# SiLU and GELU as single ScalarE functions in a hybrid decoder layer, with the stores of ScalarE's last results on ScalarE's queue

## The chip, the cores and the metric

The kernel runs on 1 core of one Trainium2 chip. The metric is device time in microseconds of one execution. The engines are named as in the profile: PE is TensorE's matmul stream and PEld its weight loads, DVE is VectorE, ACT is ScalarE, POOL is GpSimd, SP is SyncE, which here only issues DMAs. SPq and ACTq are the instruction streams of SP and ACT where they issue DMAs or wait. Each engine works through its own stream in program order.

## The reference

One layer on a sequence of 2048 tokens with 1024 channels, all in float32:

```python
h = rmsnorm(x, norm_w[i])
proj = h @ w_in[i]
u, z_s, q, k, v, z_a = jnp.split(proj, splits, axis=-1)      # 512 columns each
# s5_branch(u): state-space layer, 32 groups of 16 channels, 64 complex states each
y = y.reshape(bsz, s_len, SSM_WIDTH) + d_skip * uf
y = jax.nn.gelu(y)                                            # tanh form
y = y * jax.nn.sigmoid(y @ glu_w + glu_b)
y_s = y_s * jax.nn.silu(z_s)
# diff_attention(q, k, v): 4 heads, two 64-dim maps each, QK-norm, rotary, sub-norm
y_a = y_a * jax.nn.silu(z_a)
x = x + jnp.concatenate([y_s, y_a], axis=-1) @ w_out[i]
x = x + jax.nn.sigmoid(x @ ple_w_gate[i]) * (p[i] @ ple_w_proj[i])
```

silu(z) is z * sigmoid(z), which equals 0.5 * z * (1 + tanh(z/2)). gelu here is 0.5 * y * (1 + tanh(sqrt(2/pi) * (y + 0.044715 y^3))).

## The kernel before

Products in full precision are made from three passes: each operand is split into a rounded high part and the rest (names ending in h and l), and high x high, high x low and low x high are summed in PSUM. ACT makes the high part with a copy, DVE or POOL the low part with a subtraction.

There are three phases. **Phase 1**, up to about 722 us, makes the input projection and the whole state-space branch. **Phase 2**, up to about 1157 us, is attention, head by head, with the first half of the output projection as filler. **Phase 3** is the second half of the output projection, the gate and the residual.

In phase 1 the foreground loop goes over twelve blocks of 512 weight columns: u for both halves of the sequence, then for the first half k, zs, v, q, za, and for the second half zs, k, v, q, za. Each block goes over four tiles `t` of 256 tokens. Eight weight chunks of a block come in as `wraw` by a DMA that ACT's queue issues (L279), ACT scales and rounds them to `wh` (L282), DVE makes `wl` (L283). Blocks zs and u put channels on partitions (matmuls at L781, 256 columns), the others tokens (L827, 512 columns). The foreground then makes

- zs: DVE scales PSUM by the norm (L797, L806), ACT takes tanh (L799, L809), DVE finishes SiLU (L800, L810), SP stores to `zs_scr` (L801, L811). Tiles t 0 and 3 are stored one channel block at a time (128x256), tiles 1 and 2 two at a time (128x512).
- v: ACT scales, SP stores to `v_scr` (L834, L835).
- za: ACT scales (L838) and takes tanh (L840), DVE finishes (L841), ACT's queue stores to `za_scr` (L842).
- q, k: QK-norm and rotary on DVE and POOL, ACT and DVE make high and low parts into `stg` (L870, L871), SP stores both (L874, L875).

Between the tiles a generator, `ssm`, is advanced by a number of steps per tile that a list, `BGP`, gives; this is the background. Its second part goes over 32 state-space groups: `U` is loaded (L598), scaled on POOL (L599) and split; PE multiplies it (L530 into `pss`); DVE rotates, scans and rotates back with tables `tab` (L636 to L647) with copies on ACT between (L637, L638); ACT and DVE split the states into `xah`, `xal`; PE multiplies again; ACT copies the result to the one buffer `ysb` (L655) and SP stores it to `yg_scr` (L656). After each eighth group SP issues eight rearranging DRAM to DRAM copies `y_scr<-yg_scr` (L659), which need these stores. Every four groups DVE also makes the next parameters and tables (`tx`, one buffer, stored to `tab_scr` at L563; `rs`, stored to `r_scr` and read back as `M`, L578 and L582).

The third part of `ssm`, called the GLU here, goes over eight pieces of 256 tokens: `y` is loaded into a tile named `gg` (L693); ACT squares it (L696), DVE makes the cubic argument (L697), ACT takes tanh (L698), DVE finishes GELU (L699), ACT and DVE or POOL split it (L700, L701); PE multiplies by `gwh` and `gwl` (L710); ACT takes the tanh of the gate (L717), DVE multiplies (L718) and then multiplies by the SiLU gate, loaded back from `zs_scr` into `gz` (two buffers, L715, L721); SP stores to `yt_scr` (L722).

The tile framework's scheduler puts the instructions of all engines in order at build time by a timing model of its own, with the background at lower priority; the waits that tiles and DRAM tensors need are added to that order. So an edit in one place can move instructions elsewhere.

Of the kernel before, what the change touches and what calls it, by code (L numbers as in the profile page):

```python
# [24 lines left out]
L = 8  # L25
# [9 lines left out]
GK = math.sqrt(2.0 / math.pi)  # L35
GS = math.sqrt(0.044715)
ONE_MINUS = 0.8
# [18 lines left out]
GTB = 5  # L56
# [62 lines left out]
def hymba_kernel(ctx, tc, x_t, p_t, positions, norm_w, w_in, lam_re, lam_im, log_dt, b_re, b_im,  # L119
                 c_re, c_im, ssm_d, glu_w, glu_b, q_norm_w, k_norm_w, lq1, lk1, lq2, lk2,  # L120
                 subln_w, w_out, w_proj, w_gate, out):
    nc = tc.nc
    V, A, G, T = nc.vector, nc.scalar, nc.gpsimd, nc.tensor
# [74 lines left out]
    with ExitStack() as p1:  # L198
# [114 lines left out]
        def ssm():  # L313

            with tc.tile_pool(name="p1s", bufs=1) as sp:
# [50 lines left out]

                V.tensor_scalar(subw, subw, float(np.float32(ONE_MINUS)) * 0.5, None, op0=ALU.mult)
# [144 lines left out]
            with tc.tile_pool(name="ssB", bufs=2) as sp:  # L512
# [102 lines left out]
                for g in range(NG):  # L615
# [35 lines left out]
                    def behind(g=g, py=py, w=[w_[:, gs] for w_ in wc4], xa=xa):  # L651
# [4 lines left out]
                        nc.sync.dma_start(yg_scr[g].rearrange("l p c -> (l p) c"), ysb)  # L656
# [12 lines left out]
            with tc.tile_pool(name="ssC", bufs=1) as pg:  # L669
# [13 lines left out]
                for cq in range(8):  # L683
# [7 lines left out]
                    for k in range(4):  # L691
                        y = g2[k]
                        nc.sync.dma_start(y.rearrange("q (l c) -> q l c", l=L), y_scr[k * 128:k * 128 + 128, :, c0:c0 + 32])  # L693
                        t = pg.tile([128, 256], F32, name="gt", bufs=GTB)

                        A.activation(t, y, AF.Square, scale=GS)  # L696
                        V.scalar_tensor_tensor(t, t, 1.0, y, op0=ALU.add, op1=ALU.mult)  # L697
                        A.activation(t, t, AF.Tanh, scale=GK)  # L698
                        V.scalar_tensor_tensor(g2[k], t, 1.0, y, op0=ALU.add, op1=ALU.mult)  # L699
# [4 lines left out]
                    for mp in range(2):  # L704
# [7 lines left out]
                        for e in range(2):  # L712
# [4 lines left out]
                            A.activation(th, pm[:, e, :], AF.Tanh, bias=gb[:, m:m + 1], scale=0.25)  # L717
# [3 lines left out]
                            V.scalar_tensor_tensor(zv, th.rearrange("q (l c) -> q l c", l=L), 0.125, zv, op0=ALU.mult, op1=ALU.mult)  # L721
# [17 lines left out]
        for bi, (hf, kind, c0) in enumerate(blocks):  # L739
            leaving = bi == len(blocks) - 1 or blocks[bi + 1][0] != hf  # L740
            for t in range(4):
# [5 lines left out]
                if kind in ("u", "zs"):  # L747
# [25 lines left out]
                    for cb, k in order:  # L773
# [20 lines left out]
                        elif t in KOUT:  # L794

                            zz = pt.tile([128, 512], F32, name="t2")[:, :256]
                            V.tensor_tensor(zz, pm, rbc[hf][:, t * 256:t * 256 + 256], op=ALU.mult)  # L797
                            zo = pt.tile([128, 512], F32, name="t2")[:, :256]
                            A.activation(zo, zz, AF.Tanh, scale=0.5)  # L799
                            V.scalar_tensor_tensor(zo, zo, 1.0, zz, op0=ALU.add, op1=ALU.mult)  # L800
                            nc.sync.dma_start(zs_scr[cb * 128:(cb + 1) * 128, tok:tok + 256], zo)  # L801
                        elif cb % 2 == 1:

# [4 lines left out]
                            zo = pt.tile([128, 512], F32, name="t2")  # L808
                            A.activation(zo, zz, AF.Tanh, scale=0.5)  # L809
                            V.scalar_tensor_tensor(zo, zo, 1.0, zz, op0=ALU.add, op1=ALU.mult)  # L810
                            nc.sync.dma_start(  # L811
                                zs_scr[(cb - 1) * 128:(cb + 1) * 128, tok:tok + 256].rearrange("(b q) t -> q b t", q=128),
                                zo.rearrange("q (b t) -> q b t", b=2))
# [3 lines left out]
                else:  # L817
# [3 lines left out]
                    for j in range(2):  # L821
# [577 lines left out]
```

## Time and profile before

| what | value |
|---|---|
| median of 3 runs | 1454.8 us (1452.43 to 1457.49) |
| profiled execution, its own time | 1451.3 us |
| its span | 1449.6 us |
| mean granted TensorE clock | 0.992 of full speed |

The span goes from the first to the last instruction of the profiled execution; its own time is 1.7 us above it. Of phases 1 to 3, only phase 1 holds the lines that are changed, and the largest stretch of it is the 32 groups (about 190 to 505 us) and the GLU (about 505 to 665 us).

### The profile page before, as it was taken

Reading aid. Unit: us, or ns where it says so; the run is one execution under the profiler, and the core shown is the slowest. Engines: PE = TensorE matmul, PEld = TensorE weight load, DVE = VectorE, ACT = ScalarE, POOL = GpSimd, SP = SyncE. Lnnn points to the kernel's source line nnn. Section 1 sums busy time; section 2 is a strip of 40 time slices with the busy share of each in tenths; the row PEclk is TensorE's granted clock in tenths of the full one; section 3 lists DMA queues with packets and bytes.
Section 4 is the critical chain, followed back from the end, with each engine's and each line's share of the span. In section 5 each row is a group of like instructions: output and inputs, shape, how many; then the busy total and the mean of one; then the engine's idle time right before and its main releaser. Section 6 shows DMA issues by size and latency. Waiting matters only on the chain.

```text
span 1449.6 us, 27391 instructions
## 1 busy us (share of the span) xinstructions
PE 1383.4 (95%) x9602; PEld 1270.7 (88%) x9602; DVE 1066.3 (74%) x2527; ACT 767.9 (53%) x1689; POOL 521.3 (36%) x670
## 2 busy tenths in 40 slices
PE   7899899899999999999899999999998999999998
PEld 7898798778798888887699899989898999999998
DVE  8588898799798866675577867777877448666754
ACT  8443345456554555453586777767787523322231
POOL 6632500144000421331144454454434335543440
PEclk9999999999999999999999999999999999999999
DMA  7549756546765386556864653655434365132221
GB/s 248 152 109 293 209 178 191 166 145 191 245 192 165 107 240 186 138 150 203 240 176 121 164 143 117 162 149 142 127 88 161 138 231 227 59 117 81 73 74 59
DMA packets 219410, 230.34 MB, mean 159 GB/s; under 512 B 62712, under 2 KB 168328, under 8 KB 216712
## 3 DMA queue, kind: packets, MB, share of 16 engines
q1 hardware_dynamic: 203144, 199.22, 45.8%
q10 hardware_dynamic: 16128, 29.37, 6.6%
q8 instruction: 75, 1.23, 0.4%
q14 instruction: 63, 0.52, 0.1%
HBM read 152.19 MB, written 84.72 MB: 163 GB/s over the span
## 4 chain that ended last, share of the span: by engine, by line
PE 37%; DVE 5%; ACT 3%; issue 2%; DMA 2%; POOL 1%; SPq 0%; DVEq 0%; ACTq 0%; POOLq 0%
PE pg L1265 11%; PE po L1102 7%; PE pmf L931 6%; PE pss L1066 6%; PE pl L1281 3%; PE ptw L1098 3%; ACT s L1077 2%; DVE wgt L1157 1%; DVE s L1068 1%; PE pm L931 1%; DVE s L1090 1%; DMA wgr<-in_ple_w_gate_dram 1%; DVE wg L1153 0%; DMA yt_scr<-yo 0%; DMA yin<-yt_scr 0%
## 5 line engine op out<-in xcount | busy, mean ns | idle before, releaser
L827 PE MATMUL pmm<-wh,xh 128*128 128x512 f32 x512 | 198.3, 396 | 3.9 <-ACT wh L282 2.8
L827 PE MATMUL pmm<-wl,xh 128*128 128x512 f32 x512 | 200.4, 395 | 0.0
L827 PE MATMUL pmm<-wh,xl 128*128 128x512 f32 x512 | 200.0, 393 | 0.0
L1066 PE MATMUL pss<-ks,qd 128*128 128x512 f32 (+3 forms) x640 | 185.8, 388 | 10.3 <-DVE st L1068 6.3
L1077 ACT ACTIVATE s<-s,st 128x1024 f32<-128x1024 f32 (+4 forms) x192 | 171.7, 899 | 37.9 <-DVE st L1068 33.1
L1265 PE MATMUL pg<-oph,wg 128*128 128x256 f32 x896 | 164.4, 286 | 3.0 <-ACT oph L1238 2.9
L1102 PE MATMUL po<-vt,wt 128*128 128x128 f32 x1088 | 152.7, 276 | 0.8 <-ACT yo L1114 0.7
L1102 PEld LDWEIGHTS po<-vt,wt 128*128 128x128 f32 x1088 | 142.2, 192 | 7.2 <-ACT yo L1114 0.9
L1265 PEld LDWEIGHTS pg<-oph,wg 128*128 128x128 f32 x896 | 141.5, 195 | 3.4 <-ACT oph L1238 3.4
L1068 DVE CUSTOM_DVE_ANT_0 s<-pss,mk,st 128x512 f32<-128x512 f32 (+2 forms) x192 | 121.7, 652 | 24.3 <-PE pss L1066 22.9
L781 PE MATMUL pmm<-xh,wl 128*128 128x256 f32 x448 | 127.2, 287 | 2.7 <-DVE wl L283 2.6
L1265 PE MATMUL pg<-opl,wg 128*128 128x256 f32 x448 | 127.2, 285 | 1.2 <-POOL opl L1239 1.2
L781 PE MATMUL pmm<-xh,wh 128*128 128x256 f32 x448 | 123.0, 288 | 5.3 <-DVE stg L791 1.5
L781 PE MATMUL pmm<-xl,wh 128*128 128x256 f32 x448 | 125.8, 284 | 0.0
L1066 PEld LDWEIGHTS pss<-ks,qd 128*128 128x128 f32 x640 | 100.4, 192 | 22.8 <-DVE st L1068 11.6
L827 PEld LDWEIGHTS pmm<-wh,xh 128*128 128x128 f32 x512 | 96.1, 188 | 25.3 <-ACT wh L282 5.7
L827 PEld LDWEIGHTS pmm<-wl,xh 128*128 128x128 f32 x512 | 96.5, 188 | 19.2 <-DVE wl L283 1.5
L827 PEld LDWEIGHTS pmm<-wh,xl 128*128 128x128 f32 x512 | 96.5, 189 | 18.6
L931 PE MATMUL pmf<-yh,woh 128*128 128x256 f32 x352 | 104.8, 298 | 4.7 <-DVE x L1188 3.8
L1068 DVE CUSTOM_DVE_ANT_0 s<-pss,mk 128x512 f32<-128x512 f32 (+3 forms) x128 | 78.6, 630 | 34.3 <-PE pss L1066 28.6
L931 PE MATMUL pmf<-yh,wol 128*128 128x256 f32 x352 | 99.8, 284 | 0.0
L931 PE MATMUL pmf<-yl,woh 128*128 128x256 f32 x352 | 99.6, 283 | 0.0
(385 smaller groups left out, 3822.6 us busy)
## 6 DMA issues: line engine op xcount, KB each, us to landing
wraw<-in_w_in_dram ACTq DMA_DIRECT2D x96, 256.0 KB
xraw<-in_x_t_dram SPq DMA_DIRECT2D x40, 256.0 KB
tab<-tab_scr SPq DMA_DIRECT2D x64, 136.0 KB
qd<-qh_scr SPq DMA_DIRECT2D x64, 128.0 KB
qd<-ql_scr SPq DMA_DIRECT2D x64, 128.0 KB
xr<-in_x_t_dram SPq DMA_DIRECT2D x32, 256.0 KB
yin<-yt_scr SPq DMA_DIRECT2D x16, 512.0 KB
xp_scr<-xp SPq DMA_DIRECT2D x32, 256.0 KB
```

Source lines behind the costliest of these rows:

```text
L781: T.matmul(pm, lhsT=w[b_][:, cb * 128:cb * 128 + 128], rhs=xt[a_][:, k, :], start=(k == 0 and n == 0), stop=(k == 7 and n == 2))
L827: T.matmul(pm, lhsT=xt[a_][:, k, j * 128:j * 128 + 128], rhs=w[b_], start=(k == 0 and n == 0), stop=(k == 7 and n == 2))
L931: T.matmul(pm[:, e, :], lhsT=w[k][b_][:, ms], rhs=y[a_][:, k, :], start=(k == 0 and n == 0), stop=(k == 3 and n == 2))
L1066: T.matmul(pss[:, :cl], lhsT=qd[:, e, m, tq], rhs=ks[m][:, c0:c0 + cl], start=e == 0, stop=e == 1)
L1068: V.tensor_tensor_reduce(sr[m][pi][:, o:o + cl], pss[:, :cl], mk[:, end - cl:end], scale=1.0, scalar=3.4e38 if ci == 0 else st[:, 2 * ci - ...
L1077: A.activation(sr[m][pi][:, :cl], sr[m][pi][:, :cl], AF.Exp, bias=st[:, ci + m:ci + m + 1], scale=-1.0, accum_out=st[:, 12 + 2 * pi + m:13 ...
L1090: V.scalar_tensor_tensor(s0, s1, st[:, 11:12], s0, op0=ALU.mult, op1=ALU.add)
L1098: T.transpose(ptw[:, k, :], blocks_[kg + k], ident)
L1102: T.matmul(po[:, 0:128], lhsT=wt[:, k, :], rhs=vt[:, kg + k, :], start=kg + k == 0, stop=kg + k == len(blocks_) - 1)
L1157: V.tensor_tensor(t_, a_, b_, op=ALU.subtract)
L1265: T.matmul(banks[mp][:, e], lhsT=wg[n][k][b_][:, m * 128:m * 128 + 128], rhs=x_[a_][:, k], start=k == 0 and q == 0, stop=k == 3 and q == 2)
L1281: T.matmul(banks[mp][:, e], lhsT=wp[k][b_][:, m * 128:m * 128 + 128], rhs=p_[a_][:, k], start=(k == 0 and q == 0), stop=(k == 1 and q == 2))
```

## The change

zs: the tanh and the DVE product become one ACT function, `Silu`, in place; the store goes to ACT's queue. The tile for the second result is gone. za of the first half: `Silu` straight from PSUM with the norm as its scale. za of the second half stays with tanh, with the scale halved by a small POOL operation. GELU: the square, the two DVE products and the tanh become one ACT function, `Gelu_apprx_tanh`, in place; the constants of the gate and the sub-norm are adapted, since zs and za are no longer twice SiLU. The stores of `yg_scr`, `zs_scr`, `v_scr` and of the high parts of q and k go from SP's queue to ACT's.

```diff
-                V.tensor_scalar(subw, subw, float(np.float32(ONE_MINUS)) * 0.5, None, op0=ALU.mult)
+                V.tensor_scalar(subw, subw, float(np.float32(ONE_MINUS)), None, op0=ALU.mult)
...
                         A.copy(ysb, py)
-                        nc.sync.dma_start(yg_scr[g].rearrange("l p c -> (l p) c"), ysb)
+                        nc.scalar.dma_start(yg_scr[g].rearrange("l p c -> (l p) c"), ysb)
...
-                        A.activation(t, y, AF.Square, scale=GS)
-                        V.scalar_tensor_tensor(t, t, 1.0, y, op0=ALU.add, op1=ALU.mult)
-                        A.activation(t, t, AF.Tanh, scale=GK)
-                        V.scalar_tensor_tensor(g2[k], t, 1.0, y, op0=ALU.add, op1=ALU.mult)
+                        A.activation(y, y, AF.Gelu_apprx_tanh)
                         A.copy(gh[k], g2[k])
...
-                            A.activation(th, pm[:, e, :], AF.Tanh, bias=gb[:, m:m + 1], scale=0.25)
+                            A.activation(th, pm[:, e, :], AF.Tanh, bias=gb[:, m:m + 1], scale=0.5)
...
                             V.tensor_tensor(zz, pm, rbc[hf][:, t * 256:t * 256 + 256], op=ALU.mult)
-                            zo = pt.tile([128, 512], F32, name="t2")[:, :256]
-                            A.activation(zo, zz, AF.Tanh, scale=0.5)
-                            V.scalar_tensor_tensor(zo, zo, 1.0, zz, op0=ALU.add, op1=ALU.mult)
-                            nc.sync.dma_start(zs_scr[cb * 128:(cb + 1) * 128, tok:tok + 256], zo)
+                            A.activation(zz, zz, AF.Silu)
+                            nc.scalar.dma_start(zs_scr[cb * 128:(cb + 1) * 128, tok:tok + 256], zz)
...
-                            nc.sync.dma_start(v_scr[rows, :], vo)
+                            nc.scalar.dma_start(v_scr[rows, :], vo)
                         elif kind == "za":
-                            zz = pt.tile([128, 512], F32, name="t2")
-                            A.activation(zz, pm, AF.Copy, scale=rstd[:, ti:ti + 1])
                             zo = pt.tile([128, 512], F32, name="t2")
-                            A.activation(zo, zz, AF.Tanh, scale=0.5)
-                            V.scalar_tensor_tensor(zo, zo, 1.0, zz, op0=ALU.add, op1=ALU.mult)
+                            if hf == 0:
+                                A.activation(zo, pm, AF.Silu, scale=rstd[:, ti:ti + 1])
+                            else:
+                                rsth = pt.tile([128, 16], F32, name="qst")
+                                G.tensor_scalar(rsth[:, j:j + 1], rstd[:, ti:ti + 1], 0.5, None, op0=ALU.mult)
+                                zz = pt.tile([128, 512], F32, name="t2")
+                                A.activation(zz, pm, AF.Copy, scale=rsth[:, j:j + 1])
+                                A.activation(zo, zz, AF.Tanh)
+                                V.scalar_tensor_tensor(zo, zo, 1.0, zz, op0=ALU.add, op1=ALU.mult)
                             nc.scalar.dma_start(za_scr[rows, :], zo)
...
-                        nc.sync.dma_start(hi_s[:, :, tok:tok + 256].rearrange("h q t -> q h t"), sh_.bitcast(F32))
+                        nc.scalar.dma_start(hi_s[:, :, tok:tok + 256].rearrange("h q t -> q h t"), sh_.bitcast(F32))
```

The 128x512 stores of zs are changed in the same way as the 128x256 ones.

The first place is ACT's stream where the GLU begins (row text: line, operation, out<-in, size of the output). Of before:

```order
L680 CAST gwh<-gg 128x256
L696 ACTIVATE gt<-gg 128x256
L279 DMA wraw<-in_w_in_dram 128x512
L696 ACTIVATE gt<-gg 128x256 x2
L279 DMA wraw<-in_w_in_dram 128x512
L696 ACTIVATE gt<-gg 128x256
L698 ACTIVATE gt<-gt 128x256 x4
L700 CAST gh<-gg 128x256 x4
```

and of the change, where lines are numbered anew (`gg<-gg` at L692 is the GELU, L693 the copy to the high part, L838 the square of the QK-norm):

```order
L677 CAST gwh<-gg 128x256
L692 ACT_TABLE_LOAD
L692 ACTIVATE gg<-gg 128x256
L693 CAST gh<-gg 128x256
L692 ACTIVATE gg<-gg 128x256
L693 CAST gh<-gg 128x256
L692 ACTIVATE gg<-gg 128x256
L838 ACTIVATE t_7009<-pmm,rstd 128x512
L693 CAST gh<-gg 128x256
```

One table load has come in ahead of the first GELU, and each GELU is followed by its copy, with no DVE result between them. In ACT's whole stream there are 7 table loads against 5: this one, and one ahead of the first exponential of phase 2.

The second place is SP's stream at the rearranging copies after the 24th group. Of before:

```order
L656 DMA yg_scr<-ysb 128x256
L602 DMA tab<-tab_scr_98 64x544
L659 DMA y_scr<-yg_scr 128x1x256 x8
L656 DMA yg_scr<-ysb 128x256
L563 DMA tab_scr_99<-tx 128x544
L578 DMA r_scr_68<-rs 128x64
L602 DMA tab<-tab_scr_98 64x544 x2
L582 DMA M<-r_scr_68 128x8x64
L811 DMA zs_scr<-t_6103 128x2x256
L811 DMA zs_scr<-t_6157 128x2x256
```

and of the change (L656 is now the copies, L575 and L579 the store and the load of `r_scr`):

```order
L599 DMA tab<-tab_scr_98 64x544 x2
L656 DMA y_scr<-yg_scr 128x1x256 x8
L575 DMA r_scr_68<-rs 128x64
L560 DMA tab_scr_99<-tx 128x544
L599 DMA tab<-tab_scr_98 64x544
L579 DMA M<-r_scr_68 128x8x64
L599 DMA tab<-tab_scr_98 64x544
L595 DMA U<-ug_scr 128x256
```

The stores of ACT's results are gone from SP; the copies, the store of `rs` and the load of `M` stay, and `r_scr` now follows the copies at once.

The third place is ACT's stream in the first zs block and the groups beside it, of the change (L790 and L797 are Silu, L791 and L798 its stores, L652 and L653 the copy to `ysb` and its store):

```order
L797 ACTIVATE t_3030<-t_3030 128x512
L634 COPY sw<-pss 64x256
L635 ACTIVATE sw<-pss 64x256
L521 CAST xah<-md 128x256
L798 DMA zs_scr<-t_3030 128x2x256
L521 CAST wah<-pss 128x512
L652 COPY ysb<-pss 128x256
L653 DMA yg_scr<-ysb 128x256
L797 ACTIVATE t_3082<-t_3082 128x512
```

Before, the same piece had no DMA in it. The stores stand up to three instructions behind the result that they store, among the copies of the rotation.

## Rows read from the trace of the kernel before

**Rows 1.** The page's first part: busy time, share of the span, instructions.
```profile
PE 1383.4 (95%) x9602; PEld 1270.7 (88%) x9602; DVE 1066.3 (74%) x2527; ACT 767.9 (53%) x1689; POOL 521.3 (36%) x670
```

**Rows 2.** Busy time by stretch: PE, PEld, DVE, ACT, POOL; clock, DMA share, GB/s.
```profile
150.00:505.00 355.00, 335.26 (x2008) 292.11 (x2007) 308.68 (x689) 184.83 (x391) 79.09 (x93) 1.00 0.59 179
505.00:665.00 160.00, 155.43 (x881) 133.90 (x880) 109.33 (x247) 81.05 (x188) 44.87 (x48) 1.00 0.65 180
```

**Rows 3.** Waits of PE from 150 to 505 us: total, times, longest.
```profile
PE pss L530 <- ACT ysb L655: 3.2, 3, 2.6
PE pss L530 <- DVE wal L525: 3.1, 1, 3.1
PE pss L530 <- DVE xal L525: 2.9, 6, 0.8
PE ptr L868 <- DVE stg L871: 2.0, 1, 2.0
...
PE pmm L781 <- DVE wl L283: 1.8, 2, 1.1
```

**Rows 4.** Waits of PE from 505 to 665 us: total, times, longest.
```profile
PE pss L710 <- ACT gh L700: 2.1, 2, 1.6
PE pss L710 <- POOL gl L701: 1.1, 1, 1.1
PE pmm L827 <- ACT wh L282: 1.1, 2, 0.7
```

**Rows 5.** Groups in phase 1: shapes, count, busy us, mean ns, idle before.
```profile
L699 DVE SCALAR_TENSOR_TENSOR gg<-gt,gg 128x256 f32<-128x256 f32 x32 | 13.2, 448 | 0.7 <-ACT gt L698 0.4
L697 DVE SCALAR_TENSOR_TENSOR gt<-gt,gg 128x256 f32<-128x256 f32 x32 | 13.0, 442 | 0.6 <-ACT gt L696 0.2
...
L841 DVE SCALAR_TENSOR_TENSOR t<-t,t 128x512 f32<-128x512 f32 x16 | 11.0, 688 | 8.4 <-ACT t L840 8.4
...
L800 DVE SCALAR_TENSOR_TENSOR t<-t,t 128x256 f32<-128x256 f32 x16 | 7.1, 446 | 0.0
...
L810 DVE SCALAR_TENSOR_TENSOR t<-t,t 128x512 f32<-128x512 f32 x8 | 5.5, 683 | 0.0
...
L696 ACT ACTIVATE gt<-gg 128x256 f32<-128x256 f32 x32 | 11.8, 415 | 9.3 <-DVE gz L721 7.5 <-DMA gg<-y_scr 1.0 <-DVE gg L699 0.7
...
L840 ACT ACTIVATE t<-t 128x512 f32<-128x512 f32 x16 | 10.1, 630 | 2.3 <-DMA tab<-tab_scr 2.1
```

**Rows 6.** Timeline at the second GLU piece, DVE and PE: start, duration, idle before.
```profile
543.63 0.62 DVE L721 SCALAR_TENSOR_TENSOR gz<-gt,gz 128x256 f32<-128x256 f32 x1 [5.63 <-DMA gz<-zs_scr]
544.16 0.76 DVE L699 SCALAR_TENSOR_TENSOR gg<-gt,gg 128x256 f32<-128x256 f32 x2
...
545.07 0.50 PE L710 MATMUL pss<-gh,gwh 128*128 128x256 f32 x2 [1.65 <-ACT gh L700]
```

**Rows 7.** Timeline of SP after the 8th group, and of DVE and PE behind it.
```profile
269.73 2.65 SPq L659 DMA_DIRECT2D y_scr<-yg_scr  x4
272.48 0.40 SPq L656 DMA_DIRECT2D yg_scr<-ysb  x1
272.98 0.37 SPq L563 DMA_DIRECT2D tab_scr<-tx  x1
...
278.66 0.72 DVE L558 TENSOR_TENSOR tx<-pt 128x544 f32<-128x544 f32 x1 [7.29 <-DMA tab_scr<-tx]
...
280.74 0.36 PE L530 MATMUL pss<-Uh,wah 128*128 128x256 f32 x1 [3.06 <-DVE wal L525]
```

**Rows 8.** Timeline of SP and PE after the 24th group.
```profile
439.66 5.45 SPq L659 DMA_DIRECT2D y_scr<-yg_scr  x8
445.21 0.40 SPq L656 DMA_DIRECT2D yg_scr<-ysb  x1
445.71 0.37 SPq L563 DMA_DIRECT2D tab_scr<-tx  x1
446.18 0.41 SPq L578 DMA_DIRECT2D r_scr<-rs  x1
...
455.33 0.39 PE L530 MATMUL pss<-Uh,wah 128*128 128x256 f32 x1 [2.60 <-ACT ysb L655]
```

**Rows 9.** The stores that ACT issues already: duration ns min/median/max.
```profile
L842 ACTq DMA_DIRECT2D za_scr<-t x16: 326/326/352, 364.4 to 714.0; - x16
```

**Rows 10.** Timeline of ACT at a table load, and at the first exponential of phase 2.
```profile
184.66 0.38 ACT L638 ACTIVATE sw<-pss 64x256 f32<-64x256 f32 x1
185.05 1.28 ACT L799 ACT_TABLE_LOAD   x1
186.35 0.42 ACT L799 ACTIVATE t<-t 128x256 f32<-128x256 f32 x1
...
684.69 0.40 ACT L1077 ACTIVATE s<-s,st 128x128 f32<-128x128 f32 x1 [4.23 <-DVE st L1068]
```

**Rows 11.** Waits of ACT from 150 to 665 us, the longest.
```profile
ACT wh L282 <- DMA wraw<-in_w_in_dram: 39.8, 23, 5.8
```

More of the change, by code (lines that the diff above doesn't have):

```diff
@@ L34 @@
 TWO_PI = 2.0 * math.pi
-GK = math.sqrt(2.0 / math.pi)
-GS = math.sqrt(0.044715)
 ONE_MINUS = 0.8
@@ L693, in ssm @@
                         nc.sync.dma_start(y.rearrange("q (l c) -> q l c", l=L), y_scr[k * 128:k * 128 + 128, :, c0:c0 + 32])
-                        t = pg.tile([128, 256], F32, name="gt", bufs=GTB)
-                        A.activation(t, y, AF.Square, scale=GS)
-                        V.scalar_tensor_tensor(t, t, 1.0, y, op0=ALU.add, op1=ALU.mult)
-                        A.activation(t, t, AF.Tanh, scale=GK)
-                        V.scalar_tensor_tensor(g2[k], t, 1.0, y, op0=ALU.add, op1=ALU.mult)
+                        A.activation(y, y, AF.Gelu_apprx_tanh)
                         A.copy(gh[k], g2[k])
@@ L716, in ssm @@
                             th = pg.tile([128, 256], F32, name="gt", bufs=GTB)
-                            A.activation(th, pm[:, e, :], AF.Tanh, bias=gb[:, m:m + 1], scale=0.25)
+                            A.activation(th, pm[:, e, :], AF.Tanh, bias=gb[:, m:m + 1], scale=0.5)
                             V.scalar_tensor_tensor(th, th, 1.0, g2[m], op0=ALU.add, op1=ALU.mult)
                             zv = zs.rearrange("q (c l) -> q l c", l=L)
-                            V.scalar_tensor_tensor(zv, th.rearrange("q (l c) -> q l c", l=L), 0.125, zv, op0=ALU.mult, op1=ALU.mult)
+                            V.scalar_tensor_tensor(zv, th.rearrange("q (l c) -> q l c", l=L), 0.5, zv, op0=ALU.mult, op1=ALU.mult)
                             nc.sync.dma_start(yt_scr[cq][m * 128:m * 128 + 128, :], zs)
@@ L807, in hymba_kernel @@
                                             rbc[hf][:, t * 256:t * 256 + 256].unsqueeze(1).to_broadcast([128, 2, 256]), op=ALU.mult)
-                            zo = pt.tile([128, 512], F32, name="t2")
-                            A.activation(zo, zz, AF.Tanh, scale=0.5)
-                            V.scalar_tensor_tensor(zo, zo, 1.0, zz, op0=ALU.add, op1=ALU.mult)
-                            nc.sync.dma_start(
+                            A.activation(zz, zz, AF.Silu)
+                            nc.scalar.dma_start(
                                 zs_scr[(cb - 1) * 128:(cb + 1) * 128, tok:tok + 256].rearrange("(b q) t -> q b t", q=128),
-                                zo.rearrange("q (b t) -> q b t", b=2))
+                                zz.rearrange("q (b t) -> q b t", b=2))
                     if kind == "u" and last_t:
```

2 lines of the change are left out of this document (removed).

## The prediction

> **What bounds the kernel now.** I read the page's busy times first. PE is busy for 1383.4 of 1449.6 us, DVE for 74% and ACT for 53% of the span [rows 1]. So whatever the change saves on DVE, ACT or SP is worth only what PE stops waiting for; the matmuls themselves stay.
>
> Next I read busy time by stretch, for the stretches of phase 1 in which changed lines run [rows 2]. From 150 to 505 us, where the groups of the state-space layer run behind the k, zs, v, q and za blocks, DVE is busy for 308.68 of 355 us (87%), and PE idles 355 - 335.26 = 19.7 us (5.6%). From 505 to 665 us, the GLU, DVE is at 109.33 of 160 us (68%), and PE idles 4.6 us (2.9%). The two together, 24.3 us, are the most that this change can win there. Matmul ends are modelled, so PE loses somewhat more than these figures at each gap; I stay with the rows.
>
> Then PE's waits by who ended them. In the first stretch the named ones end on DVE (`wal` 3.1, `xal` 2.9, `stg` 2.0, `wl` 1.8 us) and on ACT's copy to `ysb` (3.2) [rows 3]; in the second on the high and low parts of GELU (2.1 and 1.1) and on the weights (1.1) [rows 4]. The last view is the timeline around the longest of these, to see what stands behind the engine that is named.
>
> **DVE and ACT work removed.** 32 + 32 products of GELU (13.0 + 13.2 us), 16 + 8 of zs (7.1 + 5.5) and 8 of the 16 of za (8 x 0.688 = 5.5) leave DVE: 44.3 us. ACT loses 32 squares (11.8) and the 8 tanh of za in the first half (8 x 0.630 = 5.0), 16.8 us in all; the other tanh become Silu and Gelu, which I cost like the tanh of their size [rows 5]. I take three effects from this and from the stores.
>
> **GELU no longer passes through DVE.** At 543 us DVE waits 5.63 us in a gate product (L721) for `gz`, and the last product of GELU (L699) is queued behind it; ACT's `gh` then ends a PE wait of 1.65 us [rows 6], and POOL's `gl` behind it ends one of 1.1 us [rows 4]. In the changed order GELU and its copy follow each other on ACT, so neither stands behind L721. The gain is 1.65 + 1.1 = 2.7 us. The bounds are nothing (ACT itself can be queued behind a wait for the matmul) and 4.3 us, all of rows 4.
>
> **SP's queue.** Behind the rearranging copies SP issues the store of `ysb`, and then what the next groups need. After the 8th group that store's slot is 272.48 to 272.98 us; `tab_scr<-tx` goes out right behind it, its landing ends a DVE wait of 7.29 us, and DVE's `wal` ends a PE wait of 3.06 us [rows 7]. Without the slot this chain is 0.50 us earlier. After the 24th group the slot is 445.21 to 445.71 and the store of `rs` stands two places behind [rows 8]; `M` is loaded from it, ACT waits for `M` with the `ysb` copy queued behind, and that ends the PE wait of 2.60 us. In the change `rs` goes out right behind the copies, so 446.18 - 445.21 = 0.97 us earlier. Together 1.5 us. The bounds are nothing and the whole 5.7 us; I stay at the slots, because the copies themselves (5.45 us in one go) stay on SP ahead of all that. The other stores that leave SP take no such place in front of a wait of PE that I could find, and cost and gain nothing there; what hides them is SP's own waiting for ACT and DVE.
>
> **DVE is less full.** In the first stretch 7.1 + 5.5 + 5.5 = 18.1 us of DVE work go, 5.1 points of its 87%. Between the two stretches PE's idle share falls by 2.7 points for 18.7 points of DVE [rows 2], so by 0.144 for one; 5.1 x 0.144 = 0.73% of 355 us, 2.6 us. The bounds are nothing, since the new order also moves the groups forward, and 2.9 + 2.0 + 1.8 = 6.7 us, the DVE waits that I have not counted yet [rows 3].
>
> **What ACT takes on.** 88 stores (32 `yg_scr`, 24 `zs_scr`, 16 `v_scr`, 16 high parts). One that ACT issues now takes 326 ns [rows 9], so 28.7 us of ACT's stream. Two table loads of 1.28 us make 2.6. Net: 28.7 + 2.6 - 16.8 = 14.5 us more. Each store waits for a result of ACT itself, at the longest for the end of the instruction before; behind it are queued the copies of the rotation (`sw`, `xah`), for which DVE waits. ACT is busy for 184.8 + 81.1 = 265.9 of 515 us [rows 2], and the 6.4 us of PE waits that it ends [rows 3, 4] are 2.4% of that, so 14.5 us cost 0.35 us. Above, each store of `ysb` could stand in the groups' chain: 32 x 0.326 = 10.4 us. I take 0.35, since ACT has 249 us of idle time there as cover.
>
> The rows show that a table load costs ACT 1.28 us, with the next instruction right behind it [rows 10]. The Trainium skill (ScalarE: Activation LUTs, section What ACT_TABLE_LOAD costs) gives a switch a second part, a drain, and some 2.66 us in all. By that two loads would cost 5.3 us of ACT time instead of 2.6; the trace shows no drain, and I go by it. The second load stands ahead of the first exponential of phase 2, where ACT idles 4.23 us for DVE [rows 10]; if that cover were gone it would cost its 1.28 us.
>
> The small POOL operations for za of the second half cost nothing: POOL is busy for 36% of the span [rows 1], and what hides them is the spare PSUM buffer that PE fills meanwhile. Without that cover the last two, which stand behind the mask of phase 2, would hold ACT's scaling and the evacuation behind it. Phases 2 and 3 hold the same instructions, somewhat reordered. No row prices that; I take nothing, and bound it by the spread of the three runs, 5.1 us either way.
>
> **The sum.** -2.7 - 1.5 - 2.6 + 0.35 = -6.45 us on an execution of 1451.3 us, so 1444.9. That execution lies 3.5 us below the median of the three runs, 1454.8; carried over to the median: 1448.4, and I say 1448. 0.3%, about what a measurement of this kernel can tell from no change, is 4.4 us, so faster means below 1450.4 and slower above 1459.2.
>
> **Rivals.**
>
> *Nothing to be seen.* PE works in order, and the scheduler has placed the groups earlier in its stream on the strength of the freed DVE time. Then DVE is as full as before while they last, the waits come at other places with the same sum, and the earlier end of the GLU is worth nothing, since no wait of PE at the end of phase 1 hangs on it. For it: only waits count, and PE idles just 24.3 us in both stretches. Against it: the wait at 543 us has lost its cause. Between 1451 and 1459, say 1454.
>
> *Slower: weights behind stores.* Before, ACT's queue carried the weights and the 16 `za_scr` stores alone. Now the stores of a block's last tile, 256 to 512 KB, stand in it ahead of the next block's weights, of which each chunk is 256 KB. ACT already waits 39.8 us for `wraw` in these stretches, in 23 waits [rows 11]. At 179 GB/s [rows 2] one more 256 KB ahead is 1.46 us; ten block switches, from k of the first half on, make 14.6 us if PE pays them all. Then 1448.4 + 14.6 = 1463. It beats the gains from 0.65 us a switch, and shows as slower from 1.1 us. Against it: only 1.1 us of PE's waits in rows 4 end on `wh`, with eight chunks of weights in SBUF.
> The Trainium skill (DMA: Bandwidth & Descriptors, section Queues, rings and completion order) says that each DMA engine takes a queue's descriptors in ring order and goes round-robin between queues; that speaks for this rival. No row here shows how the queues share an engine.
>
> *All of it.* DVE slack, the freed SP queue and the direct GELU take away every PE wait counted: 4.3 + 5.7 + 6.7 = 16.7 us, so 1438. For it: these waits are chains through all the engines that get lighter. Against it: the copies that block SP stay.
>
> **Numbers.** The forecast (1445 to 1451) 0.40, all of it 0.13, nothing to be seen 0.28, weights behind stores or another new wait on ACT 0.19. Of the forecast, 0.03 lies above 1450.4. So faster 0.50, same 0.31, slower 0.19. The likeliest time is 1448. The range goes from the full gain, 1438, up over the whole of the second case and a start of the slower one, to 1460; beyond lie about 0.04 below and 0.15 above. As both signs hold much of the chance: the forecast's own range is 1445 to 1451.
>
> **What would show it.** Right: no PE wait in the GLU ended by GELU's high or low parts; the waits after the 8th and 24th group about 0.5 and 1 us shorter; DVE's busy time lower by about 44 us; 7 table loads of 1.28 us, none with PE waiting behind; ACT's waits for `wraw` as long as now. PE's idle time from the start of the groups to the end of the GLU should fall by some 6 us. Wrong: PE waits on `wh` at block switches with long `wraw` landings; PE waits on `xah` behind a store on ACT; or a change that sits in phase 2, which I took as unmoved.

## The result, and the profile after

The changed kernel is slower: 1470.84 us (median of 4 runs, 1465.33 to 1471.86) against 1453.62 us (4 runs, 1451.22 to 1457.49), a ratio of 1.0109, interval 1.0079 to 1.0139. Its profiled execution took 1465.33 us with a span of 1463.6, 14.0 us above the one of before. It is the fastest of the four, so the profile shows 14 of some 17 us.

The page's first part, as [rows 1]:

```profile
PE 1392.5 (95%) x9602; PEld 1279.6 (87%) x9602; DVE 1033.1 (71%) x2431; ACT 759.1 (52%) x1651; POOL 523.2 (36%) x678
```

PE executes the same 9602 matmuls, yet is busy 9.1 us longer, and idles 71.1 us instead of 66.2. The mean granted clock fell from 0.992 to 0.987; (1 - 0.987) x 1463.6 = 19.0 against (1 - 0.992) x 1449.6 = 11.6, so some 7.4 of the 9.1 us are matmuls at the lower clock.

Where is it lost? The matmuls of one source line, with duration min/median/max and the first and last start, give marks. First the scores of phase 2 and the gate of phase 3 in the kernel before:

```profile
L1066 PE MATMUL pss<-ks,qd x640: 222/393/688, 683.9 to 1136.7; 128*128 128x512 f32 x100, 128*128 128x256 f32 x28, 128*128 128x384 f32 x28, 128*128 128x128 f32 x4
L1265 PE MATMUL pg<-oph,wg x896: 280/283/580, 1231.4 to 1442.7; 128*128 128x256 f32 x180
```

and in the changed one, whose lines are numbered anew:

```profile
L1059 PE MATMUL pss<-ks,qd x640: 221/393/774, 682.9 to 1145.3; 128*128 128x512 f32 x100, 128*128 128x256 f32 x28, 128*128 128x384 f32 x28, 128*128 128x128 f32 x4
L1258 PE MATMUL pg<-oph,wg x896: 278/283/553, 1245.0 to 1457.1; 128*128 128x256 f32 x180
```

The first score matmul comes 1.0 us earlier (682.9 against 683.9). That lead was there before a changed instruction ran: the first store that the change moves goes out at 147.9 us, and the first matmul of the k block, which opens the line below, starts at 114.2 us before and at 113.2 us in the changed kernel:

```profile
L827 PE MATMUL pmm<-wh,xh x512: 387/389/628, 114.2 to 704.3; 128*128 128x512 f32 x171
L814 PE MATMUL pmm<-wh,xh x512: 387/389/505, 113.2 to 701.9; 128*128 128x512 f32 x171
```

From there to the first score matmul it is 569.7 us in both: all that the prediction worked out is worth nothing there. From the first score to the last gate matmul it is 1457.1 - 682.9 = 774.2 us, against 758.8 before: 15.4 us more, in phases of which the diff changes no line (the last za tiles of phase 1 still run beside the first scores). (Of the expectations below, that of e4 counts to the end of the span, so 765.7 and 780.7; the others count the last matmul to its end, so 759.2 and 774.6.)

What differs there is the order in which the scheduler put the instructions. Only some four fifths of the 5056 PE rows of phases 2 and 3 stand in the same sequence (3924 by each instruction's place in the two programs; 4095 by tile and shape in the two traces). The first difference on SP is small. Before, with `qd` the queries and `ks`, `vt` the keys and values of a head:

```
369 L1040 DMA zg<-za_scr 128x2x128
370 L1023 DMA qd<-qh_scr 64x2x256
371 L1014 DMA ks_8858<-kh_scr 64x512
372 L1014 DMA ks_8858<-kl_scr 64x512
```

and in the change, where more of the second step's queries get ahead of the keys, and the order differs from there on:

```
281 L1033 DMA zg<-za_scr 128x2x128
282 L868 DMA ql_scr<-stg 128x4x256
283 L1016 DMA qd<-qh_scr 64x2x256 x2
284 L1007 DMA ks_8674<-kh_scr 64x512
```

PE's waits from 690 to 1250 us in the changed kernel (total, times, longest):

```profile
PE pss L1059 <- DMA qd<-qh_scr: 7.8, 3, 3.3
...
PE po L1095 <- ACT yo L1107: 3.2, 1, 3.2
```

Before, the first of these was

```profile
PE pss L1066 <- DMA qd<-qh_scr: 1.8, 2, 1.2
```

The longest of the three is at 1114.55 us. SP's timeline in front of it (`yt_scr<-yo` stores an attention result, `yin` loads such results for the output projection), and PE's row:

```profile
1097.01 0.42 SPq L1108 DMA_DIRECT2D yt_scr<-yo  x1
1107.15 0.37 SPq L909 DMA_DIRECT2D yin<-yt_scr  x1
...
1109.40 0.61 SPq L1016 DMA_DIRECT2D qd<-qh_scr  x1
...
1114.55 1.01 PE L1059 MATMUL pss<-ks,qd 128*128 128x384 f32 x2 [3.28 <-DMA qd<-qh_scr]
```

SP stands 10 us between its store and the load of `yin`, which by the profile waits for a store of `yt_scr` to land (9.6 us), and the queries, which need nothing of it, stand behind. Before, the same load stood behind the queries, and no wait of PE from 1100 to 1130 us ended on a load of them:

```profile
1109.99 0.58 SPq L1023 DMA_DIRECT2D qd<-qh_scr  x1
...
1112.62 0.54 SPq L916 DMA_DIRECT2D yin<-yt_scr  x1
```

At 905 us it is ACT: the copy of `yin` to its high part stands ahead of exponentials and waits 3.60 us for the load; PE waits 3.20 us behind. In each of the three places the clock falls as well. The changed kernel around the one at 825 us, in pieces of 2 us (columns as in [rows 2]):

```profile
822.00:824.00 2.00, 0.00 (x0) 0.00 (x0) 0.46 (x4) 2.00 (x6) 0.00 (x0) 0.98 0.79 189
824.00:826.00 2.00, 1.00 (x3) 0.84 (x4) 0.00 (x0) 2.00 (x5) 0.00 (x0) 0.50 0.94 222
826.00:828.00 2.00, 2.00 (x7) 1.62 (x6) 1.82 (x5) 2.00 (x11) 1.53 (x4) 0.50 0.36 105
828.00:830.00 2.00, 2.00 (x11) 2.00 (x11) 2.00 (x8) 0.30 (x2) 1.44 (x3) 0.50 0.19 66
```

PE stands still for 3 us; towards the end of that the clock falls to 0.50 (1.2 GHz), and it stays there while PE is busy again. The three places in windows, changed kernel, then before:

```profile
820.00:850.00 30.00, 26.98 (x190) 25.32 (x189) 16.11 (x54) 20.22 (x49) 10.72 (x19) 0.89 0.50 144
900.00:925.00 25.00, 20.68 (x144) 19.29 (x143) 16.30 (x42) 17.25 (x43) 13.56 (x22) 0.93 0.30 91
1100.00:1130.00 30.00, 26.64 (x188) 24.20 (x187) 25.53 (x65) 22.16 (x53) 13.76 (x23) 0.94 0.49 156
```

```profile
820.00:850.00 30.00, 28.92 (x227) 27.50 (x226) 22.82 (x67) 21.82 (x54) 13.38 (x25) 1.00 0.58 163
900.00:925.00 25.00, 25.00 (x191) 23.47 (x189) 19.52 (x56) 18.64 (x52) 15.99 (x28) 1.00 0.53 139
1100.00:1130.00 30.00, 28.14 (x233) 27.31 (x232) 21.01 (x57) 18.40 (x48) 13.29 (x28) 1.00 0.50 178
```

PE runs 190, 144 and 188 matmuls there instead of 227, 191 and 233. It idles 10.7 us in the three windows, against 2.9 before, and the lower clock is worth up to 0.11 x 30 + 0.07 x 25 + 0.06 x 30 = 6.9 us: by this estimate the three places hold up to 7.8 + 6.9 = 14.7 of the 15.4 us.

### The profile page after: what moved, and what is told of

Its sections match the earlier page's. It is cut to its first block, busy times and chain, and to the rows that moved or that the text cites. A ratio compares the mean times of both kernels' runs of the same rounds, so it can differ in the third digit from the quotient of the medians.

```text
span 1463.6 us, 27202 instructions
## 1 busy us (share of the span) xinstructions
PE 1392.5 (95%) x9602; PEld 1279.6 (87%) x9602; DVE 1033.1 (71%) x2431; ACT 759.1 (52%) x1651; POOL 523.2 (36%) x678
## 4 chain that ended last, share of the span: by engine, by line
PE 49%; DMA 18%; DVE 16%; ACT 5%; POOL 5%; issue 5%; SPq 2%; ACTq 0%; DVEq 0%; POOLq 0%
PE pg L1258 11%; PE pmf L924 7%; PE po L1095 7%; PE pss L1059 6%; PE pmm L814 6%; PE ptw L1091 3%; PE pl L1274 3%; DMA tab_scr<-tx 2%; PE pmm L774 2%; DMA wraw<-in_w_in_dram 2%; DMA gz<-zs_scr 2%; PE pm L924 2%; DMA xraw<-in_x_t_dram 1%; POOL qst L842 1%; DVE wl L281 1%
## 5 line engine op out<-in xcount | busy, mean ns | idle before, releaser
L1095 PEld LDWEIGHTS po<-vt,wt 128*128 128x128 f32 x1088 | 142.5, 195 | 11.6 <-ACT yo L1107 3.4
L1059 PEld LDWEIGHTS pss<-ks,qd 128*128 128x128 f32 x640 | 101.9, 193 | 25.7 <-DVE st L1061 10.7
```

The lines of the kernel that those rows point to most:

```text
L1059: T.matmul(pss[:, :cl], lhsT=qd[:, e, m, tq], rhs=ks[m][:, c0:c0 + cl], start=e == 0, stop=e == 1)
L1095: T.matmul(po[:, 0:128], lhsT=wt[:, k, :], rhs=vt[:, kg + k, :], start=kg + k == 0, stop=kg + k == len(blocks_) - 1)
```

## The experiments

Theory A: the order of phases 2 and 3 costs the time, whatever moved it there. Theory B: the stores on ACT's queue do. Theory C: the functions do. The table has all runs. "Same" counts the PE rows of phases 2 and 3 (of 5056) that stand in before's sequence and in the changed kernel's; "score" is the first score matmul, "rest" the time from it to the last start of the gate's `pg<-oph` matmuls, both in the profiled execution and read as in the rows above. Ratios, with their interval, are to the runs of before made beside each: median 1453.6 us for the changed kernel, 1455.6 for e1 to e4, 1455.7 for e5 to e8, 1455.5 for e9 to e11, 1454.9 for e12.

| run | same as before / changed | score | rest | median us | ratio |
|---|---|---|---|---|---|
| before | 5056 / 3924 | 683.9 | 758.8 | 1453.6 | |
| changed | 3924 / 5056 | 682.9 | 774.2 | 1470.8 | 1.0109 (1.0079 to 1.0139) |
| e1 v stores | 3928 / 5039 | 684.8 | 771.2 | 1466.3 | 1.0082 (1.0054 to 1.0109) |
| e2 zs stores | 5056 / 3924 | 693.1 | 759.9 | 1462.6 | 1.0047 (1.0028 to 1.0067) |
| e3 functions | 3924 / 5054 | 694.9 | 773.1 | 1474.6 | 1.0149 (1.01 to 1.0197) |
| e4 GELU | 4110 / 3902 | 694.5 | 764.0 | 1466.6 | 1.0077 (1.0048 to 1.0106) |
| e5 order back | 4795 / 4108 | 687.9 | 763.0 | 1458.6 | 1.0023 (1.0002 to 1.0044) |
| e6 order only | 3932 / 4051 | 685.6 | 763.2 | 1464.7 | 1.0065 (1.0044 to 1.0086) |
| e7 stores | 3941 / 5033 | 692.9 | 773.8 | 1473.1 | 1.0133 (1.01 to 1.0165) |
| e8 yo store | 3952 / 3984 | 684.2 | 768.6 | 1464.7 | 1.0071 (1.0046 to 1.0095) |
| e9 copies on POOL | 4795 / 4108 | 684.4 | 757.9 | 1455.4 | 0.9996 (0.9979 to 1.0012) |
| e10 rs on POOL | 4795 / 4108 | 684.7 | 764.1 | 1454.5 | 1.0002 (0.9977 to 1.0027) |
| e11 functions, order back | 4795 / 4106 | 693.8 | 765.0 | 1466.7 | 1.0076 (1.0057 to 1.0096) |
| e12 both on POOL | 4795 / 4108 | 683.3 | 760.3 | 1456.5 | 1.0006 (0.9991 to 1.0022) |

Over the whole table the rest goes with the order: 758.8 and 759.9 us in before's, 771.2 to 774.2 in the changed kernel's (but for a few rows), whether stores, functions or both were changed, and 757.9 to 765.0 in that of e5, which five kernels share but for a few rows.

**e1, v's stores alone.**

```diff
-                            nc.sync.dma_start(v_scr[rows, :], vo)
+                            nc.scalar.dma_start(v_scr[rows, :], vo)
```

> The kernel before with one edit: the 16 stores of v go from SP's queue to ACT's. In its program the instructions of phases 2 and 3 stand almost as in the changed kernel (5039 of 5056 PE rows in the same sequence) and not as before (3928 of 5056). Theory A, the order of phases 2 and 3 costs the time: first score matmul within 2 us of before's 683.9 us, end of phase 2 and the gate's first matmul 8 to 15 us later than before (1155.8 and 1231.4), time 1461 to 1470 us. Theory B, stores on ACT's queue delay weights and copies in phase 1: 16 of 88 stores, so 16/88 of 17 us, 3 us, time 1455 to 1459, and the delay is there by the first score matmul. Theory C, the functions on ACT cost it: no change, 1451 to 1456.

Theory A. Sixteen stores of phase 1 leave the first score matmul where it was and bring nearly the whole loss behind it:

```profile
L1066 PE MATMUL pss<-ks,qd x640: 220/393/767, 684.8 to 1143.1; 128*128 128x512 f32 x100, 128*128 128x256 f32 x28, 128*128 128x384 f32 x28, 128*128 128x128 f32 x4
```

**e2, zs's stores alone.** The same edit on the two stores to `zs_scr`.

> The kernel before with one edit: the 24 stores of zs go from SP's queue to ACT's. In its program all 5056 PE rows of phases 2 and 3 stand in before's sequence. Theory A (order of phases 2 and 3): no change, 1451 to 1457 us, pauses of PE after the first score matmul as before. Theory B (stores on ACT's queue): 24/88 of 17 us, so 4.6 us more, 1456 to 1461, in phase 1. Theory C (functions): no change.

With before's sequence the rest is as before, as A says; but the time is 7 us up, all ahead of the first score matmul, as B says, and above B's range. Of the 9.2 us there, 2.4 stand already at the k block (116.6 us), before a store of zs. PE's waits hold little of the rest. Those for `wh` (L827) are the longest by their sum from 150 to 690 us, but before they were nearly the same, four in both:

```profile
PE pmm L827 <- ACT wh L282: 3.4, 4, 1.2
```

```profile
PE pmm L827 <- ACT wh L282: 2.8, 4, 1.4
```

From the k block to the first score matmul PE idles 27.3 us, 2.0 more than before, and is busy 4.8 us longer, at a lower granted clock, as these windows show, before and then e2:

```profile
114.20:683.90 569.70, 544.40 (x3130) 469.98 (x3128) 453.19 (x1093) 283.36 (x606) 133.62 (x153) 1.00 0.63 186
116.60:693.10 576.50, 549.19 (x3129) 474.18 (x3126) 452.87 (x1093) 283.98 (x606) 140.31 (x153) 0.99 0.62 184
```

So moving these stores alone has a price in phase 1 too, the larger part of it in matmuls that take longer. PE's sequence in phase 1 departs from before's at 195 us, so whether the queue or that new order brings it is open.

**e3, the functions alone**: the changed kernel with all five lines of stores back on `nc.sync`.

> The change without its stores: Silu and Gelu as in the changed kernel, all 88 stores back on SP's queue. Phases 2 and 3 stand in the changed kernel's sequence (5054 of 5056 PE rows). Theory A: 1462 to 1472 us, first score matmul at 680 to 685 us, the loss after it. Theory B: the gains of the prediction without the loss, 1445 to 1452. Theory C: 1465 to 1472 with the loss before the first score matmul.

The rest is the changed kernel's, as A says; and phase 1 is 11 us longer, as C says. Each theory has half of the loss, and 1474.6 us is above both ranges. After the 8th group the chain of [rows 7] is there again, DVE's wait for `tx` and PE's behind it:

```profile
278.44 0.73 DVE L555 TENSOR_TENSOR tx<-pt 128x544 f32<-128x544 f32 x1 [7.35 <-DMA tab_scr<-tx]
...
281.15 0.55 PE L527 MATMUL pss<-Uh,wah 128*128 128x256 f32 x1 [3.52 <-DVE wal L522]
```

**e4, GELU alone**: before, with `A.activation(y, y, AF.Gelu_apprx_tanh)` in place of GELU's four operations (constants adapted).

> The kernel before with GELU alone as one ACT function (Silu not used, stores on SP's queue). Phases 2 and 3 stand in a third sequence (4110 of 5056 PE rows as before, 3902 as in the changed kernel). Theory A: the first score matmul 0 to 4 us earlier than 683.9 us, and the end apart from that by whatever pauses the third sequence has; it predicts that the time after the first score matmul differs from before's 765.7 us and from the changed kernel's 780.7 us by the sum of PE's pauses and half-clock stretches there. Theory B: 1448 to 1453 us, all gain. Theory C: slower than before by 3 us or more in phase 1.

A third sequence with a rest of 764.0, and a late first score matmul, as C says: slower by 11 us where one ACT function replaces two and two DVE products. Up to the GLU PE's stream is before's, and there it is 4.0 us late already; of the 10.6 us in phase 1 those are this execution's own, and 6.6 come behind.

**e5, the order put back.** The changed kernel, in phase 2:

```diff
+            save = tc.cur_priority
+            tc.cur_priority = save - 5 * (h == 0)
             for c in range(1, 4):
                 load(c)
+            tc.cur_priority = save
```

> The changed kernel with one edit that moves no work: the loads of k and v for the first head are requested five priority steps earlier. Phase 1 stands exactly as in the changed kernel on every engine; of the 5056 PE rows of phases 2 and 3, 4795 now stand in before's sequence and 4108 in the changed kernel's. Theory A, the order of phases 2 and 3 costs the time: from the first score matmul to the end 759 to 766 us (before 759.2, changed 774.6), no pauses near 825, 905 and 1114 us, time 1455 to 1463 us. Theory B, functions and stores in phase 1 cost it, whatever the order behind: 1467 to 1473 us, with 770 us or more after the first score matmul.

Theory A: 1470.84 - 1458.57 = 12.3 us come back from an edit that moves no work, with phase 1 instruction for instruction the changed kernel's. The median is still 2.9 us above before's, just clear of noise. Of the three windows, that at 905 us is whole again; the others are not:

```profile
820.00:850.00 30.00, 27.31 (x201) 25.75 (x200) 19.42 (x56) 19.53 (x51) 12.16 (x23) 0.94 0.54 150
900.00:925.00 25.00, 25.00 (x195) 23.81 (x194) 18.82 (x57) 20.02 (x50) 15.89 (x26) 1.00 0.46 125
1100.00:1130.00 30.00, 26.25 (x206) 24.87 (x205) 24.39 (x61) 21.79 (x51) 13.82 (x22) 1.00 0.54 185
```

PE's stream is the changed kernel's well past the first pause (up to 840 us there), and the wait for queries in it is still 2.7 us. In the last window PE idles 3.75 us, but at full clock. So the expected end of all three pauses did not come; what went is the second one and most of the stretches at the lower clock.

**e6, an order and nothing else.** The kernel before; `tc.cur_priority` is 10 lower while the queries of the second step are requested.

> The kernel before with one edit that moves no work: the loads of q for the second step of the first head are requested ten priority steps earlier. Phase 1 stands exactly as before on every engine; of the 5056 PE rows of phases 2 and 3, 3932 stand in before's sequence and 4051 in the changed kernel's, so it is a sequence of its own. Theory A, such an order alone is worth as much as the whole result: first score matmul at 684 us within 5 us, the time from there differs from before's 759.2 us by 4 us or more, most likely upwards, time 1459 to 1470 us. Theory B, phases 2 and 3 take the same whatever their order: 1451 to 1459 us.

Theory A: 9 us slower by the median (1464.65 against 1455.69), with no instruction of phase 1 touched. (The profiled execution is the fastest of ten, 1457.4 us.)

**e7, all stores and no function.**

> The kernel before with all 88 stores on ACT's queue, and none of the functions. Phases 2 and 3 stand in the changed kernel's sequence (5033 of 5056 PE rows). Theory A: 771 to 776 us after the first score matmul. With e1 (the same sequence, 16 stores moved, 1466.3 us) as base: if the stores help in phase 1, as the step from the functions alone (1474.6) to the full change (1470.8) suggests, 1460 to 1466 us; if they cost, as the 24 stores of zs alone did (7 us), 1470 to 1480 us.

They cost when alone: phase 1 is 9 us longer, and the rest is the changed kernel's. Here PE does wait for weights, 6.2 us against 2.8 before (the row shown at e2), and ACT waits 48.9 us for `wraw` from 150 to 690 us, against 41.6. From the k block on PE idles 2.0 us more than before and is busy 6.0 us longer:

```profile
PE pmm L827 <- ACT wh L282: 6.2, 4, 3.5
...
115.20:692.90 577.70, 550.42 (x3128) 475.38 (x3126) 456.13 (x1095) 283.50 (x606) 134.72 (x153) 0.99 0.62 184
```

**e8, one store more.** The changed kernel, with attention's result stored by ACT:

```diff
-                nc.sync.dma_start(yt_scr[i][512 + h * 128:640 + h * 128, :], yo)
+                nc.scalar.dma_start(yt_scr[i][512 + h * 128:640 + h * 128, :], yo)
```

> The changed kernel with one more store moved from SP's queue to ACT's: that of attention's result to yt_scr in phase 2, which ACT makes last. Phases 2 and 3 come out in yet another sequence (3952 of 5056 PE rows as before, 3984 as in the changed kernel). Theory H, the pauses of phase 2 are loads of q held up on SP behind stores that wait for other engines: PE's waits that end on q loads fall from 8.0 us to under 3, 760 to 768 us after the first score matmul, time 1455 to 1464. Rival, the loads are late for another reason or ACT's exponentials are held up in their place: 1467 to 1475 us.

Half right. PE's waits for the high parts of the queries fall from 7.8 to 1.2 us and 6 us come back, but part of the wait moves to ACT (that for `wt` was 2.0 us), and both the 768.6 us and the time lie just above theory H's ranges:

```profile
PE po L1095 <- ACT wt L1093: 4.0, 4, 1.9
PE pmf L924 <- ACT xp L983: 3.8, 1, 3.8
...
PE pss L1059 <- DMA qd<-qh_scr: 1.2, 1, 1.2
```

The sequence changed as well, so the 6 us are not the store's alone.

**e9 and e10, SP freed further.** e5 with, in e9, `nc.gpsimd` in place of `nc.sync` for the copies `y_scr<-yg_scr`, and in e10 for `r_scr<-rs`.

> The kernel of e5 (the changed kernel with phases 2 and 3 nearly in before's sequence) with the 32 rearranging copies y_scr<-yg_scr on POOL's queue in place of SP's; phases 2 and 3 stand as in e5. In the changed kernel SP issues eight of them from 431.7 to 437.5 us, the store of rs goes out at 438.6, and PE waits 3.3 us at 447.5 for the copy to ysb that is queued on ACT behind M. Theory S, SP's copies are what keeps phase 1 from gaining: no PE wait above 1.5 us after the 24th group, first score matmul 3 to 6 us earlier than in e5 (687.9), time 1450 to 1456 us. Rival, the wait is the round trip through r_scr and the copies only move the hold-up to POOL, behind which U is scaled: 1457 to 1466 us.

> The kernel of e5 with the eight stores of rs to r_scr on POOL's queue in place of SP's, so that they no longer stand behind the rearranging copies; phases 2 and 3 stand as in e5. Theory S: M comes 2.5 us earlier after the 24th group (rs was ready at 436.1 us, its store went out at 438.6), time 1454 to 1458 us. Rival, store and load take their 8 us of round trip anyway and the group order moves: 1457 to 1463 us, as e5 within what can be measured.

Both times are as theory S has it: e9 is 3.2 us below e5, e10 4.1 us, and both equal the kernel before. The intervals overlap that of e5, though, and the mechanism is not shown. In e9 the longest wait of PE from 395 to 470 us is 2.0 us, for DVE's `xal`, above the 1.5 expected. The first score matmuls, at 684.4 and 684.7 us, lie among the 682.9 to 687.9 that the changed kernel's phase 1 took in three executions, and 5.1 us of e9's profiled gain lie behind it, where its order is e5's. From the end of `rs` to the copy of `M` on ACT it is 10.7 us in e5, 8.8 in e9 and 9.8 in e10: 0.9 us earlier in e10, not 2.5.

**e11, the functions with the order of e5.**

> The functions without the stores (as e3), with e5's one edit to the priority of the first head's loads, so that phases 2 and 3 stand nearly in before's sequence (4795 of 5056 PE rows). Theory A: the step from e3 is the same as from the changed kernel to e5, 12 us, so 1460 to 1465 us, 759 to 766 us after the first score matmul. If the functions cost nothing by themselves in phase 1, 1452 to 1459 us, and e3's late first score matmul (694.9) was one execution's.

8 us come back from e3, not 12, and the first score matmul at 693.8 repeats e3's 694.9: the functions without the stores do cost phase 1 some 10 us. The time lies above both ranges.

**e12, e9 and e10 together.**

> The kernel of e5 with both edits of e9 and e10: the rearranging copies and the stores of rs on POOL's queue; phases 2 and 3 stand as in e5. The candidate for a version that beats both kernels. If the gains in phase 1 add up, the pauses after the 24th group go altogether and it is 2 to 5 us below e9 and before: 1450 to 1453 us. Rival: PE's pauses come back at other places of phase 1, as they did between the changed kernel and before: 1453 to 1458 us, no difference from before that can be measured.

The rival: nothing on top. No kernel that ran beats the one before.

## Why the prediction was wrong, step by step

**The step that failed** is "Phases 2 and 3 hold the same instructions, somewhat reordered. No row prices that; I take nothing, and bound it by the spread of the three runs, 5.1 us either way." The reordering was the result: 15.4 us in the profiled execution, 12.3 us by the medians of e5, and 9 us for another order on the kernel before (e6). The spread of one program's runs bounds its noise, not what another order of it takes. The three places show how: loads of queries and of `yin` came late, PE stopped, and the clock fell behind it. That the order changes could be read beforehand; what it costs could not, and the range should have been wider for it.

**GELU no longer through DVE (-2.7 us).** The DVE product is gone, the wait is not. ACT now stands in GELU itself for the load of `y`:

```profile
576.26 0.42 ACT L692 ACTIVATE gg<-gg 128x256 f32<-128x256 f32 x1 [5.66 <-DMA gg<-y_scr]
...
578.33 0.39 PE L703 MATMUL pss<-gh,gwh 128*128 128x256 f32 x1 [1.73 <-ACT gh L693]
```

PE's waits for `gh` from 505 to 665 us are 2.4 us in 2 times, against 2.1 [rows 4]; only the one for POOL's `gl` went. What is late next is the load.

**SP's slots (-1.5 us).** The slots were not given back at either place. After the 8th group PE's wait is 0.71 us instead of 3.06 [rows 7], but not for the reason that I gave:

```profile
263.85 2.64 SPq L656 DMA_DIRECT2D y_scr<-yg_scr  x4
266.58 0.40 SPq L575 DMA_DIRECT2D r_scr<-rs  x1
267.03 0.43 SPq L560 DMA_DIRECT2D tab_scr<-tx  x1
...
271.68 0.72 DVE L555 TENSOR_TENSOR tx<-pt 128x544 f32<-128x544 f32 x1 [5.09 <-DMA tab_scr<-tx]
272.32 0.68 DVE L522 TENSOR_TENSOR wal<-pss,wah 128x512 fp32r<-128x512 f32 x1
...
273.15 0.36 PE L527 MATMUL pss<-Uh,wah 128*128 128x256 f32 x1 [0.71 <-DVE wal L522]
```

The store of `rs` has taken the slot: `tab_scr<-tx` goes out 0.54 us behind the copies, against 0.60. The chain is shorter since DVE gets on 4.65 us behind that store instead of 5.68, and since `wal` now stands right behind `tx`, with no `na` between (before, it ran at 279.30 us). After the 24th group the term was wrong in full. The chain there in the changed kernel:

```profile
431.71 5.75 SPq L656 DMA_DIRECT2D y_scr<-yg_scr  x8
438.62 0.32 SPq L575 DMA_DIRECT2D r_scr<-rs  x1
...
446.52 0.62 ACT L521 CAST mgh<-M 128x512 fp32r<-128x512 f32 x1 [6.07 <-DMA M<-r_scr]
...
447.46 0.39 PE L527 MATMUL pss<-Uh,wah 128*128 128x256 f32 x1 [3.31 <-ACT ysb L652]
```

From the end of the copies to the store of `rs` it is 438.62 - 437.46 = 1.16 us, and 1.07 us before [rows 8], with two stores in it. Nothing stands there now; by the profile SP waits 1.1 us for the copies themselves (`y_scr<-yg_scr`). The round trip through `r_scr` takes 8 us, and PE waits 3.31 us instead of 2.60.

**DVE less full (-2.6 us), and the sum in phase 1.** The stretches of [rows 2], after:

```profile
150.00:505.00 355.00, 336.82 (x1998) 291.28 (x1997) 295.17 (x654) 182.02 (x388) 80.17 (x90) 0.99 0.59 183
505.00:665.00 160.00, 156.46 (x886) 134.97 (x885) 89.55 (x187) 72.64 (x155) 40.47 (x53) 1.00 0.61 167
```

There PE's idle time falls from 24.3 to 21.7 us, 2.6 instead of some 6. From the k block to the first score matmul it idles 3.0 us less and is busy 3.0 us longer, at a lower clock, so nothing is left (before: the row at e2):

```profile
113.20:682.90 569.70, 547.44 (x3127) 470.76 (x3126) 419.19 (x997) 273.03 (x568) 132.32 (x161) 0.99 0.62 187
```

DVE's share of the first stretch fell by 3.8 points, not 5.1, and PE's idle time there by 1.6 us, where my slope of 0.144 gives 1.9; that slope was drawn through two stretches with different work, so the fit may be luck. Three executions of the changed kernel's phase 1 reach the first score matmul at 682.9, 687.9 (e5) and 684.2 (e8), two of before's at 683.9 and 685.6 (e6): no gain. My rival *nothing to be seen* described this part, mechanism included: the last GLU matmul starts at 621 us instead of 646, and no wait hangs on it. The halves are not neutral apart, though: the functions alone cost phase 1 about 10 us (e3, e11), the stores alone 9 (e7). Both halves have a PE sequence of their own in phase 1 from 190 us on or earlier, and no run moves that order alone, so it is a rival to either. For the functions the rows show part of why: PE idles 16.1 us from 150 to 330 us with the stores on SP, 12.5 before, 8.4 in the change. For the stores alone it is in part the waits for `wh` of e7; what makes PE busy longer there is open beyond the lower clock.

**What ACT takes on (+0.35 us).** Held as far as the rows go, though my 6.4 us left out waits for `mgh`, `wah`, `xah` and for `wh` ahead of the GLU: in both stretches ACT ended 11.3 us of PE's waits, and ends 12.0 in the change, 5.2 of them for `ysb` instead of 3.2. ACT's waits for weights from 150 to 665 us, against 39.8 us [rows 11]:

```profile
ACT wh L280 <- DMA wraw<-in_w_in_dram: 29.9, 28, 2.9
```

So the rival *weights behind stores* did not happen in this kernel, though its time was the nearest; PE waits for `wh` once there, 1.6 us. Its waits show in e7, where all the stores moved and DVE's products stayed. What the Trainium skill (DMA: Bandwidth & Descriptors, section Queues, rings and completion order) says of ring order and turns between queues, no run here shows. Each of the two new table loads takes 1.28 us, and the first GELU starts right behind its one:

```profile
507.20 1.28 ACT L692 ACT_TABLE_LOAD   x1 [0.99 <-DMA gg<-y_scr]
508.49 0.42 ACT L692 ACTIVATE gg<-gg 128x256 f32<-128x256 f32 x1
```

The drain that the Trainium skill adds (ScalarE: Activation LUTs, section What ACT_TABLE_LOAD costs) is not in these rows.

**The signs.** Among those for wrong was "a change that sits in phase 2, which I took as unmoved", and that is what came. Of those for right, the 7 table loads came, and ACT's waits for `wraw` are shorter than before; PE still waits for `gh`, the wait after the 24th group is longer, and DVE's busy time fell by 33.2 us, not 44.

## What to carry to other kernels

Where a scheduler orders the whole program, an edit also buys a new order of parts that it doesn't touch: compare that order before believing a sum, price it by its own measurement, and separate it from the edit by a change of priority that moves no work. Where one engine issues loads in order, look for a load that must wait for a store's landing ahead of loads that need nothing; here it held them for 10 us. Moving work off an engine that is not the bound may only move the wait to what is late next, here the load of `y`. And one execution's time up to a mark is not yet the work of an edit: compare a mark ahead of the first changed instruction too, and the granted clock.

## What the runs showed of the hardware

- Around PE's pause of 3 us at 825 us the granted clock was 0.50 from 824 to 830 us, five of these with PE busy again. A pause of 3.06 us before [rows 7] had no such drop, as this window of the kernel before shows; what sets the two apart is not shown:

```profile
275.00:300.00 25.00, 21.71 (x102) 17.11 (x101) 19.42 (x38) 12.30 (x26) 2.88 (x5) 1.00 0.68 208
```

- A store of 128 KB (`yt_scr<-yo`) issued at 1097.01 us let the load behind it, which waits for its landing, go only at 1107.15 us.
- An instruction's duration is more than what it takes of its engine: 44.3 us of DVE instructions went, and DVE's busy time fell by 1066.3 - 1033.1 = 33.2 us, 346 ns for each of the 96. Neighbours overlap, as the two rows of DVE in [rows 6] show: the second starts at 544.16, the first ends at 544.25 us.
